# Storing the plain query parts unsplit, a head per store, and splitting them in each attention block

## The chip, the cores and the metric

The kernel runs on one NeuronCore of a Trainium2 chip. The metric is the device time of one execution, in microseconds (us), as the median of several runs; lower is better.

## The reference

One inference step of a two-layer decoder: an mLSTM layer, then a layer of multi-head latent attention (MLA), each followed by a SwiGLU FFN. The change lies in the MLA layer, in the queries of the 1024 prompt tokens and in the attention that reads them:

```python
q = (rmsnorm(c_q, g_q) @ w_uq).reshape(B, S, MLA_HEADS, QK_NOPE + QK_ROPE)   # 8 heads, 128 plain + 64 rotary
q_nope = q[..., :QK_NOPE]
q_rope = rope(q[..., QK_NOPE:], pos)
...
s = q_lat . c_kv + q_rope . k_r          # per head, causal, S = 1024
p = softmax(s * MLA_SCALE)
out = p . c_kv
```

Eight more requests (the sample) each attend, with one token, over 8192 cached positions that are gathered from pages in HBM. All arithmetic is float32.

## The kernel before

TensorE multiplies float32 data as float32r parts: a value x is split into a high part (written by ScalarE as float32r) and the rest (x minus the high part, by VectorE or GpSimd). A product of two split operands is three matmuls: lines 131, 132 and 133 (`mm3`). `split` (line 110) does the two instructions at lines 114 and 115; `split_g` (line 122) is a form that copies PSUM to SBUF on ScalarE first, so that GpSimd can subtract from SBUF (lines 125 to 127).

The MLA layer's part that matters has three stages.

**Queries** (`queries`, line 1307). For each head h the plain part is `P` h: 27 matmuls into three PSUM tiles of 344 tokens ("chunks", 344, 344 and 336 of the prompt). The rotary parts of four heads at a time are `R0` and `R4`: 54 matmuls, then VectorE turns them with the cosines and sines. The order is R0 with P0, P1, P2, P3, R4 with P4, P5, P6, P7 (`ORDER`). Every result chunk is split into an SBUF tile `qx` (two parts) and stored to HBM scratch: plain parts to `qn_d` (line 1331, SP's queue for heads 0 to 3, GpSimd's for the rest), rotary parts to `qr_d` (line 1336, GpSimd's queue for heads 0 to 3, SP's for the rest; two stores for each tile, since a rotary row in `qr_d` holds both parts). There are 12 `qx` buffers and 36 `qx` tiles. `wq` is the weight of all heads (2.36 MB in three loads on SP's queue, line 1319); P1 to P7 and R4 split their weights from it into `wh` and `wl`. R0 and P0 have small loads of their own.

**Sample query** (`sample_query`, line 1406): small matmuls on the eight sample tokens (line 1419 onward, input `qnS`, the last column of each plain part) and ScalarE copies into `qbd` (line 1426). It follows the queries.

**Attention** (`attention`, line 1446). For each of 8 heads there are four blocks G of 256 queries (`prompt`, 32 blocks or slots). A block loads its queries with `load_q` (line 1464) into `q` (both plain parts) and `qrr` (rotary), two buffers each: on ScalarE's queue for head 0, on SP's for the others. Then it does scores (lines 1538 to 1545), the softmax on VectorE and ScalarE (lines 1546 to 1562), transposes and splits of the weights (line 1576 on) and the product with the values (line 1596). Beside the blocks run the next head's keys and values (`head_ops`) and the sample's units (`sample_units`, line 1659): GpSimd gathers pages (`nat`, `nrp`), VectorE transposes them (line 1693), TensorE multiplies (lines 1700 and 1725).

The order on each engine is set by a scheduler, from the order in the code, priorities and its own costs. Each engine then runs its list in order: an instruction that waits holds back all that stand behind it, and this holds for the DMAs that an engine issues.

Of the kernel before, what the change touches and what calls it, by code (L numbers as in the profile page):

```python
# [9 lines left out]
F32 = mybir.dt.float32  # L10
F32R = mybir.dt.float32r
I32 = mybir.dt.int32
AF = mybir.ActivationFunctionType
ALU = mybir.AluOpType
# [4 lines left out]
P = 128  # L19
D = 1024  # L20
KT = D // P
S = 1024
# [3 lines left out]
CW = T // NCH  # L26
# [62 lines left out]
class Kern:  # L89
# [1217 lines left out]
    def queries(self, qs, cq):  # L1307
        nc = self.nc
        V = nc.vector
        cqh, cql, rc, rn, wT = cq  # L1310
        self.qn_d = self.t(self.dp, [8, 2, P, S], "qn_d")
        self.qr_d = self.t(self.dp, [8, P, S], "qr_d")
        wuq = self.mla_w_uq[0]
        self.qnS = self.t(qs, [P, 8, NS], "qnS")
# [1 line left out]

        wq = self.t(qs, [P, 3, 8, 192], "wq")
        for k in range(3):
            nc.sync.dma_start(wq[:, k].rearrange("p h c -> p (h c)"), wuq[k * P:(k + 1) * P, :])


        def keep(c, src, dst, lo_eng=None):
            w = slice(c * CW, min((c + 1) * CW, S))
            n = w.stop - w.start
            x = self.t(qs, [P, 2, CW], "qx", F32R, bufs=12)[:, :, :n]
            self.split(x[:, 0], x[:, 1], src[:, :n], lo_eng=lo_eng)
            return lambda: dst(x.bitcast(F32), w)

        def put_n(h):
            e = nc.sync if h < 4 else nc.gpsimd  # L1330
            return lambda x, w: e.dma_start(self.qn_d[h, :, :, w].rearrange("i p s -> p i s"), x)

        def put_r(h0, e):
            def f(x, w):
# [36 lines left out]
        def plain(h):  # L1371
            raw = wq[:, :, h, 0:P]
            if h == 0:
                raw = self.t(self.wp, [P, KT * P], "wr")[:, : 3 * P].rearrange("p (k m) -> p k m", m=P)
                nc.scalar.dma_start(raw, self.wsrc(wuq, 0, 3, 0, P))
            w = [self.t(self.wp, [P, KT * P], x, F32R)[:, : 3 * P].rearrange("p (k m) -> p k m", m=P) for x in ("wh", "wl")]
            self.split(w[0], w[1], raw)

            def ev(c, cs, ps):
                stores.append(keep(c, ps, put_n(h)))  # L1380
                if c == NCH - 1:
                    V.tensor_tensor(self.qnS[:, h], ps[:, CW - NS:], self.rqS, op=ALU.mult)

            def chunk(c):
                self.linear(w, (cqh, cql), 3, P, ev, chunks=(c,))
                self.lastq = self.last
            return chunk

        stores = []
        for op in ORDER.split():  # L1390
            h = int(op[1:] or 0)
# [54 lines left out]
    def attention(self, ckh, ckl, kk, kl, cqp, cq):  # L1446
        nc = self.nc
# [12 lines left out]
            return r  # L1460

        late = []

        def load_q(h, G):
            g = slice(G * 256, G * 256 + 256)
            q = self.t(pe, [P, 2, 256], "q", F32R, bufs=2)
            x = self.t(pe, [P, 256], "qrr", F32R, bufs=2)
            e = nc.scalar if h == 0 else nc.sync
            e.dma_start(q.bitcast(F32), self.qn_d[h, :, :, g].rearrange("i p s -> p i s"))
            e.dma_start(x.bitcast(F32), self.qr_d[h, :, g])  # L1470
            return q, x

        def head_ops(h):
# [44 lines left out]
        def prompt(h, G, kt, vt):  # L1518
            hv = slice((h % 2) * P, (h % 2) * P + P)
            nk = 2 * G + 2  # L1520
            q, qx = load_q(h, G)
            pt = []
            pn = []
            for i in (2 * G, 2 * G + 1):
                n = (i + 1) * P
# [3 lines left out]
                qs = slice((i % 2) * P, (i % 2) * P + P)  # L1529
# [3 lines left out]
                for c in range(nb):  # L1533
                    w = min(512, n - c * 512)
# [29 lines left out]
            for j0 in range(0, nk, 4):  # L1564
# [3 lines left out]
                for j2 in range(0, m, 2):  # L1568
                    ps = ps1().rearrange("p (j q) -> p j q", q=256)
# [16 lines left out]
            ps = ps1()  # L1586
# [16 lines left out]
        qs = self.pool("qs", side="right")  # L1603
# [13 lines left out]
        for h in range(8):  # L1617
# [11 lines left out]
            for i, G in enumerate(range(4) if h % 2 == 0 or h == 7 else range(3, -1, -1)):  # L1629
                slot = h * 4 + i  # L1630
# [15 lines left out]
        ps = self.tp()  # L1646
# [268 lines left out]
```

## Time and profile before

| what | value |
|---|---|
| median of 3 runs | 2748.43 us (2739.51 to 2748.51) |
| profiled execution | 2769.77 us, 0.78% above the median |
| its span, first to last instruction | 2766.9 us |
| mean granted TensorE clock | 0.972 of full speed |
| busy: PE, PEld, DVE, ACT, POOL | 94%, 88%, 54%, 43%, 32% of the span |
| HBM | 255.17 MB read, 125.70 MB written |
| software queue (GpSimd's), hardware queues | 180.99 MB; 183.61 and 16.36 MB |

PE is TensorE's matmuls and PEld its weight loads, DVE is VectorE, ACT is ScalarE, POOL is GpSimd, SP is SyncE, whose queue only issues DMAs; ACTq and SPq are the DMA issues of those engines. In the rows of the timeline the first column is the start and the second the duration, and brackets give the idle time of the engine ahead of the instruction and what ended it. All times of one view are us from the start of the span. The queries of the MLA layer lie at 1339 to 1411, the attention at 1411 to 1912.

### The profile page before, as it was taken

What the parts mean: (1) busy time and instruction counts of PE and PEld (TensorE: products, weight loads), DVE (VectorE), ACT (ScalarE), POOL (GpSimd) and SP (SyncE); (2) the same over time, 40 slices, a digit from 0 to 9 for tenths busy, and PEclk for the clock granted to TensorE, in tenths of its full rate; (3) what the DMA queues carried; (4) which work ended last, traced back from release to release, by engine and by line L of the source; (5) the groups of instructions that cost most, each with busy time, mean ns of one, the idle gap of its engine ahead of it and who ended that gap; (6) DMA issues with size and microseconds to landing.
All of it is one profiled execution on the core that took longest, in us unless ns stands there. A gap on an engine that the chain in (4) does not pass through costs nothing.

```text
span 2766.9 us, 51992 instructions
## 1 busy us (share of the span) xinstructions
PE 2587.6 (94%) x20719; PEld 2440.0 (88%) x20719; DVE 1491.9 (54%) x3217; ACT 1177.6 (43%) x2651; POOL 875.0 (32%) x843
## 2 busy tenths in 40 slices
PE   8999988989999999999878888898988999999998
PEld 8998877989999999999765667676888999999998
DVE  4345578863334334465546786677574444334455
ACT  4212334544444444453244455546344444444442
POOL 1001002243333333332235444442223333333343
PEclk9999989999999999999889999999999999999999
DMA  5133455426655565453666676654533656555653
GB/s 184 39 76 95 128 140 136 133 69 130 127 118 116 115 123 119 89 178 111 195 209 239 212 249 230 223 204 141 170 100 87 127 116 125 116 117 117 117 138 102
DMA packets 344936, 384.27 MB, mean 139 GB/s; under 512 B 24361, under 2 KB 296110, under 8 KB 336374
## 3 DMA queue, kind: packets, MB, share of 16 engines
q0 software_dynamic: 42064, 180.99, 27.5%
q1 hardware_dynamic: 278422, 183.61, 22.7%
q10 hardware_dynamic: 24208, 16.36, 2.3%
q8 instruction: 162, 2.65, 0.4%
q14 instruction: 80, 0.66, 0.1%
HBM read 255.17 MB, written 125.70 MB: 138 GB/s over the span
## 4 chain that ended last, share of the span: by engine, by line
PE 68%; DVE 13%; DMA 8%; issue 4%; ACT 4%; POOL 2%; SPq 0%; another core or an unknown queue 0%; POOLq 0%; ACTq 0%; DVEq 0%
PE sc L133 10%; PE sc L131 10%; PE sc L132 10%; PE mm L131 5%; PE mm L133 5%; PE mm L132 5%; PE ss L131 5%; PE ss L132 5%; PE ss L133 5%; DVE tt L1693 3%; PE ss L1725 2%; DMA Gb<-G_d 2%; PE ss L1700 2%; DVE wl L115 1%; PE mm L1596 1%
## 5 line engine op out<-in xcount | busy, mean ns | idle before, releaser
L131 PE MATMUL ss<-ah,dh 128*128 128x344 f32 x864 | 277.0, 321 | 6.7 <-ACT st L1075 6.3
L1075 ACT COPY st<-ss 128x344 f32<-128x344 f32 x432 | 189.9, 441 | 214.2 <-PE ss L133 184.1
L132 PE MATMUL ss<-al,dh 128*128 128x344 f32 x864 | 277.0, 321 | 1.9 <-POOL al L115 1.9
L133 PE MATMUL ss<-ah,dl 128*128 128x344 f32 x864 | 276.2, 320 | 0.0
L114 ACT ACTIVATE wh<-wr 128x512 fp32r<-128x512 f32 (+2 forms) x152 | 126.1, 830 | 228.9 <-PE mm L132 130.6
L1077 POOL DMA_DIRECT2D x_d<-st x144 | 124.5, 864 | 241.7 <-ACT st L1075 234.8
L131 PEld LDWEIGHTS ss<-ah,dh 128*128 128x128 f32 x864 | 162.6, 188 | 7.7 <-ACT st L1075 6.7
L132 PEld LDWEIGHTS ss<-al,dh 128*128 128x128 f32 x864 | 163.0, 189 | 2.4 <-POOL al L115 2.4
L115 POOL TENSOR_TENSOR al<-u,ah 128x512 fp32r<-128x512 f32 (+1 forms) x84 | 118.1, 1406 | 148.3 <-ACT ah L114 148.2
L115 DVE TENSOR_TENSOR wl<-S,wl 128x512 fp32r<-128x512 f32 x89 | 78.1, 877 | 157.0 <-ACT wl L114 122.6
L133 PEld LDWEIGHTS ss<-ah,dl 128*128 128x128 f32 x864 | 162.6, 188 | 0.0
L1693 DVE STREAM_TRANSPOSE tt<-nat 128x1024 f32<-128x1024 f32 x128 | 154.0, 1223 | 12.9 <-PE ss L1700 6.3
L115 DVE TENSOR_TENSOR wh<-S,wh 128x512 fp32r<-128x512 f32 x91 | 68.6, 754 | 119.4 <-ACT wh L114 91.2
L1041 DVE TENSOR_TENSOR u<-u,sc 128x260 f32<-128x260 f32 (+1 forms) x168 | 70.8, 421 | 114.7 <-PE sc L133 113.4
L115 DVE TENSOR_TENSOR wl<-wr,wh 128x1024 fp32r<-128x1024 f32 (+2 forms) x83 | 100.5, 1212 | 42.4 <-ACT wh L114 34.8
L1007 POOL TENSOR_TENSOR S<-S,wr 128x512 f32<-128x512 f32 x45 | 62.9, 1397 | 175.3 <-DVE wh L115 87.9
L1700 PE MATMUL ss<-tt,qbd 128*32 128x128 f32 x2560 | 95.6, 285 | 22.5 <-DVE tt L1693 13.7
L1000 POOL TENSOR_TENSOR S<-wr 128x512 f32<-128x512 f32 x45 | 62.0, 1378 | 164.7 <-DMA wr<-in_ffn_w_gate_up_dram 151.5
L131 PE MATMUL mm<-zh,wh 128*128 128x344 f32 x320 | 105.3, 329 | 7.8 <-DVE ot L459 7.8
L1700 PEld LDWEIGHTS ss<-tt,qbd 128*32 128x32 f32 x2560 | 73.7, 114 | 39.1 <-DVE tt L1693 21.2
L115 DVE TENSOR_TENSOR dl<-dr,dh 128x256 fp32r<-128x256 f32 x144 | 69.2, 480 | 72.0 <-ACT dh L114 72.0
L132 PE MATMUL mm<-zl,wh 128*128 128x344 f32 x320 | 104.5, 327 | 0.0
(919 smaller groups left out, 9268.4 us busy)
## 6 DMA issues: line engine op xcount, KB each, us to landing
x_d<-st POOLq DMA_DIRECT2D x144, 516.0 KB
wr<-in_ffn_w_gate_up_dram SPq DMA_DIRECT2D x98, 512.0 KB
dr<-in_ffn_w_down_dram SPq DMA_DIRECT2D x144, 128.0 KB
wr<-in_mlstm_w_in_dram SPq DMA_DIRECT2D x24, 512.0 KB
wr<-in_mlstm_w_out_dram SPq DMA_DIRECT2D x16, 512.0 KB
wr<-in_mla_w_o_dram SPq DMA_DIRECT2D x15, 512.0 KB
q<-qn_d SPq DMA_DIRECT2D x28, 256.0 KB
x_d<-x SPq DMA_DIRECT2D x16, 260.0 KB
```

The costliest lines, as they stand in the source:

```text
L114: ins = nc.scalar.activation(hi, src, AF.Copy)
L115: self.low = e.tensor_tensor(lo, src, hi.bitcast(F32), op=ALU.subtract)
L131: mm(ps, wh, xh, start=start, stop=False, **kw)
L132: mm(ps, wh, xl, start=False, stop=False, **kw)
L133: self.last = mm(ps, wl, xh, start=False, stop=stop, **kw)
L1000: G(s, a21, a22, op=ALU.add)
L1007: G(s, s, a11, op=ALU.subtract)
L1041: V.tensor_tensor(u[:, 1], u[:, 1], ps, op=ALU.add)
L1075: nc.scalar.copy(st[:, cs], ps)
L1077: nc.gpsimd.dma_start(self.x_d[:, d], st, accum_op=ALU.add)
L1693: V.transpose(out=tt, in_=src.rearrange("p s (c i) -> p c s i", i=32))
L1700: nc.tensor.matmul(psS[32 * j:32 * j + 32, u * P:u * P + P], self.qbd[:, b, cb], tt[:, c, 4 * j:4 * j + 4].rearrange("p s k -> p (s k)"), ...
```

## The change

- `qn_d` holds each head's plain part once, unsplit: 8 x 128 x 1024 floats (4 MB, before 8 MB).
- ScalarE copies the three chunks of a head from PSUM into one tile `qp` (128 x 1024, four buffers). When the last is there, the whole head goes out in one store of 128 rows of 4 KB: 8 stores in place of 24. The high part and the rest are no longer made here.
- `qx` serves the rotary parts alone, with 6 buffers in place of 12. The stores of `qr_d` are as they were.
- `load_q` reads the unsplit queries (128 rows of 1 KB) into the second half of `q`; ScalarE writes the high part to the first half (line 1474 of the changed kernel), and GpSimd subtracts in place (line 1475): two more instructions for each of 32 blocks.
- From slot 1 on, the code of a block calls `load_q` for the next block ahead of its own scores; `q` has two buffers as before.
- The three loads of `wq` are issued by GpSimd, no longer by SP.

```diff
-        self.qn_d = self.t(self.dp, [8, 2, P, S], "qn_d")
+        self.qn_d = self.t(self.dp, [8, P, S], "qn_d")
...
-            nc.sync.dma_start(wq[:, k].rearrange("p h c -> p (h c)"), wuq[k * P:(k + 1) * P, :])
+            nc.gpsimd.dma_start(wq[:, k].rearrange("p h c -> p (h c)"), wuq[k * P:(k + 1) * P, :])
...
-            x = self.t(qs, [P, 2, CW], "qx", F32R, bufs=12)[:, :, :n]
+            x = self.t(qs, [P, 2, CW], "qx", F32R, bufs=6)[:, :, :n]
...
-        def put_n(h):
-            e = nc.sync if h < 4 else nc.gpsimd
-            return lambda x, w: e.dma_start(self.qn_d[h, :, :, w].rearrange("i p s -> p i s"), x)
...
+            x = self.t(qs, [P, S], "qp", bufs=4)
             def ev(c, cs, ps):
-                stores.append(keep(c, ps, put_n(h)))
+                w = slice(c * CW, min((c + 1) * CW, S))
+                nc.scalar.copy(x[:, w], ps[:, :w.stop - w.start])
                 if c == NCH - 1:
+                    stores.append(lambda: (nc.sync if h < 4 else nc.gpsimd).dma_start(self.qn_d[h], x))
...
-            e.dma_start(q.bitcast(F32), self.qn_d[h, :, :, g].rearrange("i p s -> p i s"))
+            raw = q[:, 1].bitcast(F32)
+            e.dma_start(raw, self.qn_d[h, :, g])
             e.dma_start(x.bitcast(F32), self.qr_d[h, :, g])
+            nc.scalar.activation(q[:, 0], raw, AF.Copy)
+            nc.gpsimd.tensor_tensor(q[:, 1], raw, q[:, 0].bitcast(F32), op=ALU.subtract)
...
-            q, qx = load_q(h, G)
+            slot = h * 4 + G if h % 2 == 0 or h == 7 else h * 4 + 3 - G
+            q, qx = ahead.pop(slot, None) or load_q(h, G)
+            n = slot + 1
+            if 0 < slot < 31:
+                ahead[n] = load_q(n // 4, n % 4 if n // 4 % 2 == 0 or n >= 28 else 3 - n % 4)
```

What the scheduler makes of it, at three places. The rows show line, operation and tiles (output, arrow, inputs) in the order in which the engine runs them; the numbers in names tell buffers apart.

ScalarE in the queries, before, from the third split of R0's and P0's chunks on. `qrr` and `q` are the queries of slots 0 and 1, and `wh <- wq` are the weights of P1 and P2:

```order
L114 ACTIVATE qx_14512<-rfa_14507 128x344
L1470 DMA qrr_15078<-qr_d_14414 128x256
L114 ACTIVATE qx_14520<-rfa_14515 128x344
L114 ACTIVATE qx_14533<-sc_14523 128x344
L114 ACTIVATE wh_14598<-wq_14417 128x384
L114 ACTIVATE wh_14657<-wq_14417 128x384
L1469 DMA q_15077<-qn_d_14413 128x2x256
L114 ACTIVATE qx_14561<-rfa_14556 128x336
L1470 DMA qrr_15236<-qr_d_14414 128x256
```

The same place in the changed kernel, from P2's weights (the first row; P1's stand two rows ahead of it) to P3's (the last row):

```order
L114 ACTIVATE wh_14645<-wq_14417 128x384
L1473 DMA qrr_15024<-qr_d_14414 128x256
L114 ACTIVATE qx_14572<-rfa_14567 128x336
L1472 DMA q_15023<-qn_d_14413 128x256
L1472 DMA q_15181<-qn_d_14413 128x256
L1380 COPY qp_14597<-sc_14598 128x344
L1473 DMA qrr_15182<-qr_d_14414 128x256
L1380 COPY qp_14597<-sc_14609 128x344
L1474 ACTIVATE q_15023<-q_15023 128x256
L1474 ACTIVATE q_15181<-q_15181 128x256
L1380 COPY qp_14597<-mm_14620 128x336
L114 ACTIVATE wh_14685<-wq_14417 128x384
```

The weights of P1 and P2 have moved ahead of the first query load; both loads and the splits of slots 0 and 1 now stand between them and P3's weights.

GpSimd's list at the start of the queries, before (`cn_d` is a small store of the stage ahead):

```order
L1282 DMA cn_d_14301<-so_14297 8x256
L1336 DMA qr_d_14414<-qx_14463 4x32x344 x2
L1336 DMA qr_d_14414<-qx_14471 4x32x344 x2
L1336 DMA qr_d_14414<-qx_14512 4x32x344 x2
L1336 DMA qr_d_14414<-qx_14520 4x32x344 x2
```

and in the changed kernel:

```order
L1282 DMA cn_d_14301<-so_14297 8x256
L1319 DMA wq_14417<-in_mla_w_uq_dram 128x1536 x3
L1332 DMA qr_d_14414<-qx_14464 4x32x344 x2
L1332 DMA qr_d_14414<-qx_14472 4x32x344 x2
L1332 DMA qr_d_14414<-qx_14511 4x32x344 x2
L1332 DMA qr_d_14414<-qx_14519 4x32x344 x2
```

The three loads of `wq` now stand on this queue, ahead of R0's stores.

ScalarE in the attention, before, at the end of head 1 (`wr` are softmax rows, `ot` a block's output, `vt` the next head's values):

```order
L1560 ACTIVATE wr_16512<-wr_16512,sm_16502 128x128
L1555 ACTIVATE wr_16527,sm_16517<-sc_16518,mx_16516,rqt_14290 128x256
L1560 ACTIVATE wr_16527<-wr_16527,sm_16517 128x256
L1599 COPY ot_16419<-mm_16406 128x256
L1601 DMA ot_d_14312<-ot_16419 128x256
L125 ACTIVATE vt_16422<-mm_16423 128x512
```

and in the changed kernel:

```order
L1570 ACTIVATE wr_16478<-wr_16478,sm_16468 128x128
L1750 ACTIVATE fac_16661<-fac_16661 128x1
L1570 ACTIVATE wr_16493<-wr_16493,sm_16483 128x256
L1474 ACTIVATE q_16837<-q_16837 128x256
L1609 COPY ot_16383<-mm_16370 128x256
L1611 DMA ot_d_14312<-ot_16383 128x256
L125 ACTIVATE vt_16386<-mm_16387 128x512
```

The split of a later block's queries stands ahead of the copies that empty PSUM.

More of the change, by code (lines that the diff above doesn't have):

```diff
@@ L1462, in attention @@
         late = []
+        ahead = {}
         def load_q(h, G):
```

## The prediction

> **What bounds the kernel now.** I read the page first (busy shares, granted clock, chain), then stretches of the time line around the edit, then the waits inside them.
>
> ```profile
> PE 2587.6 (94%) x20719; PEld 2440.0 (88%) x20719; DVE 1491.9 (54%) x3217; ACT 1177.6 (43%) x2651; POOL 875.0 (32%) x843
> PEclk9999989999999999999889999999999999999999
> PE 68%; DVE 13%; DMA 8%; issue 4%; ACT 4%; POOL 2%; SPq 0%; another core or an unknown queue 0%; POOLq 0%; ACTq 0%; DVEq 0%
> ```
>
> TensorE bounds the whole. The clock row dips only around the middle, where the queries and the start of the attention lie, so the edit is worth what TensorE idles, or runs slowly, there. The stretches (length, then busy us of PE, PEld, DVE, ACT, POOL with instruction counts, then granted clock, DMA share, GB/s):
>
> ```profile
> 1349.00:1357.00 8.00, 0.04 (x1) 0.00 (x0) 0.77 (x2) 1.29 (x4) 0.51 (x1) 0.65 0.68 217
> 1357.00:1366.00 9.00, 8.49 (x31) 8.05 (x32) 4.11 (x14) 0.85 (x2) 2.17 (x4) 0.55 0.58 144
> 1380.00:1396.00 16.00, 15.84 (x100) 15.56 (x100) 15.29 (x47) 6.43 (x15) 4.08 (x6) 1.00 0.65 195
> 1396.00:1411.00 15.00, 7.58 (x57) 7.49 (x55) 2.94 (x10) 2.25 (x5) 3.28 (x6) 0.84 0.57 195
> 1411.00:1430.00 19.00, 16.59 (x79) 12.99 (x79) 4.42 (x20) 11.32 (x29) 2.79 (x4) 0.68 0.38 136
> 1430.00:1912.00 482.00, 412.44 (x5083) 325.45 (x5084) 338.94 (x745) 249.65 (x660) 217.77 (x213) 0.95 0.64 219
> ```
>
> A full-speed matmul of the queries takes 16.0/100 = 0.16 us. There are two holes, 1349 to 1357 and before 1411, each followed by a stretch at about half clock. The attention itself is 86% PE-busy (412.44 of 482) and full speed. ScalarE's and TensorE's time lines name the causes:
>
> ```profile
> 1355.32 0.34 ACTq L1470 DMA_DIRECT2D qrr<-qr_d  x1
> 1355.71 0.49 ACT L114 ACTIVATE qx<-rfa 128x344 fp32r<-128x344 f32 x1 [9.01 <-DMA qr_d<-qx]
> 1366.20 0.48 ACT L114 ACTIVATE qx<-rfa 128x336 fp32r<-128x336 f32 x1 [8.02 <-DMA qr_d<-qx]
> 1409.64 0.46 ACT L114 ACTIVATE qx<-sc 128x344 fp32r<-128x344 f32 x1 [7.86 <-DMA qr_d<-qx]
> 1357.01 0.65 PE L131 MATMUL sc<-cqh,wh 128*128 128x344 f32 x1 [7.97 <-ACT wh L114]
> 1401.91 1.68 PE L1419 MATMUL ss<-qnS,wT 128*128 128x8 f32 x14
> 1411.19 4.01 PE L1419 MATMUL ss<-qnS,wT 128*128 128x8 f32 x18 [7.61 <-DVE qnS L1382]
> ```
>
> The first hole is ScalarE standing in slot 0's rotary load, which waits for R0's first-chunk stores, while P1's weight split stands behind it. At 1366 it has waited for slot 1's load in the same way. At 1409.64 it waits for a `qx` buffer whose rotary store has not landed, and P7's last pieces, with `qnS`, come late.
>
> **The change, part by part.**
>
> *First hole.* P1's weights now stand ahead of the load; they need only `wq` and the copy of P0's last chunk.
>
> ```profile
> 1340.62 2.25 SPq L1319 DMA_DIRECT2D wq<-in_mla_w_uq_dram  x3
> 1337.58 0.50 POOL L1282 DMA_DIRECT2D cn_d<-so  x1
> 1350.00:1352.00 2.00, 0.00 (x0) 0.00 (x0) 0.00 (x0) 0.00 (x0) 0.00 (x0) 0.87 1.03 364
> 1352.00:1354.00 2.00, 0.00 (x0) 0.00 (x0) 0.00 (x0) 0.00 (x0) 0.00 (x0) 0.50 0.58 127
> L114 ACT ACTIVATE qx<-sc x16: 439/457/487, 1344.5 to 1409.6; 128x344 fp32r<-128x344 f32 x16
> L115 DVE TENSOR_TENSOR qx<-sc,qx x16: 501/508/517, 1345.2 to 1410.1; 128x344 fp32r<-128x344 f32 x16
> L1331 POOL DMA_DIRECT2D qn_d<-qx x12: 725/725/761, 1381.3 to 1411.7; - x12
> ```
>
> GpSimd is free at 1338.1, 2.5 us before SP issued the same loads. Three issues of 0.73 us and 2.36 MB at 364 GB/s (6.5 us) put `wq` in SBUF near 1347. TensorE ends P0 at 1349.0; a copy and a split of some 0.45 us each give P1's start at 1350.3. The wait falls from 7.97 to 1.3: gain 6.7. The ends are 8.0 (no wait) and 4.9 (if `wq` lands only where the rate fell, at 1352, P1 starts by 1352.1).
>
> *Half clock after it.* The 31 matmuls of 1357 to 1366 took 9.0 us where 31 x 0.16 = 5.0 would do: gain 4.0 when the hole goes, 0 if another hole of that size follows.
>
> *The wait that may replace it.* P3's weights now stand behind slot 1's rotary load, which needs all eight stores of R0's chunks 0 and 1.
>
> ```profile
> 1357.15 8.60 DMA qr_d<-qx
> 1380.68 27.48 SPq L1336 DMA_DIRECT2D qr_d<-qx  x12
> 1404.00:1406.00 2.00, 0.00 (x0) 0.00 (x0) 0.00 (x0) 0.00 (x0) 0.00 (x0) 1.00 0.67 223
> 1406.00:1408.00 2.00, 0.00 (x0) 0.00 (x0) 0.00 (x0) 0.00 (x0) 0.00 (x0) 0.52 0.27 94
> 1408.00:1410.00 2.00, 0.00 (x0) 0.00 (x0) 0.00 (x0) 0.36 (x2) 0.00 (x0) 0.50 0.26 86
> ```
>
> The chain shows that the last of the eight needed 8.60 us from issue to landing. ScalarE no longer stops ahead of that chunk, so its stores are issued by about 1349.5 and land near 1358.1; the load, two copies, two query splits and the weight split (about 2.6 us) put P3 at 1360.7. TensorE has P1 and P2 meanwhile, 54 x 0.16 = 8.6 us, to 1358.9. New wait 1.8. The ends: 0, and 9.0 if the stores go one behind the other, since SP's twelve took 27.48 / 12 = 2.29 us each: eight from 1347 land at 1365.3, P3 at 1367.9. I take 1.8, because the 8.60 is the row of this very store.
>
> The Trainium skill ("DMA: Bandwidth & Descriptors", section on why a DMA increments its semaphore by 16) says that a DMA uses as many engines, at most 16, as divide its slowest dimension, which is four heads for a rotary store: the lowest four from SP, and from GpSimd four consecutive ones from a moving cursor. The trace agrees for SP: a DMA share of 0.26 and 0.27 is four engines of 16. No row here shows the cursor; by that rule GpSimd's stores run beside each other, the new wait is 0 and the sum 1.8 larger.
>
> The Trainium skill ("TensorE: Matmul & The Clock Gate", Part 1) lets the clock drop after an idle window of about 3.4 us. The trace agrees: TensorE went idle at 1403.6, the clock was 1.00 to 1406 and 0.52 after it. By that rule a wait of 1.8 costs no clock, and one of 9.0 does.
>
> *Second hole.* `qx` is used by 12 rotary tiles with 6 buffers, so R4 needs what R0 stored over 20 us before; `qp` has four buffers, and P4 to P7 need the stores of P0 to P3, which stand on SP's queue ahead of the slow rotary ones. ScalarE does not stop and the 7.61 go. The ends are 7.6 and 0 (if a `qp` store comes late). I take 7.6, since SP's queue holds nothing else then. The 18 multiplications at line 1419 took 4.01 us where 14 had taken 1.68: 1.85 from the clock alone; up to 1430 the mean clock was 0.68, at most 0.32 x 19 = 6.1. I take 3.0, nearer the lower end, because ScalarE (11.32 of 19) paces that stretch.
>
> *Work removed from the queries.* 24 subtractions of 0.51 us on VectorE (12 us) and 4 MB of stores. TensorE, at 15.84 of 16 in the stretch from 1380, covers them: 0. The 24 copies replace 24 splits on ScalarE at the same 0.45.
>
> *Work added to the attention.*
>
> ```profile
> 1422.44 0.39 ACT L114 ACTIVATE wh<-mm 128x256 fp32r<-128x256 f32 x1 [1.04 <-PE mm L1576]
> 1317.69 0.90 POOL L222 TENSOR_TENSOR rq<-rq,sq 128x344 f32<-128x344 f32 x1 [0.25 <-ACT sq L221]
> L1538 PE MATMUL sc<-kt,q 128*128 128x512 f32 (+3 forms) x72 | 29.2, 406 | 4.8 <-DMA q<-qn_d 3.3 <-ACT wr L1555 1.4
> 1784.90 5.51 DMA q<-qn_d
> 1667.51 0.36 SPq L1469 DMA_DIRECT2D q<-qn_d  x1
> 1667.86 0.30 PE L1538 MATMUL sc<-kt,q 128*128 128x128 f32 x1
> 1674.41 0.28 PE L1538 MATMUL sc<-kt,q 128*128 128x128 f32 x1
> ```
>
> 32 splits of 0.39 are 12.5 us on ScalarE; 32 subtractions of 0.90 x 256/344 = 0.67 are 21.4 us on GpSimd. Loading ahead in the code brings nothing by itself: with two buffers SP already issues a load as soon as the block before last is read (1667.51, as the block at 1667.86 begins; used at 1674.41), and one wait of 3.3 us is all that TensorE had from queries; its load took 5.51 us. What changes is that ScalarE now stands in its list until the load has landed, with PSUM copies, softmax rows and the next weights queued behind it, and GpSimd until ScalarE is done, with the gathers behind it. If neither is ever late, the loss is -3.3 (the one wait goes); if both are wholly on the path, 33.9. I take 8: ScalarE is busy 249.65 of 482 us, so 52% of its 12.5, or 6.5, delays something, and 1.5 for the few blocks as tight as the one at 1674. GpSimd I cost at 0, covered by its own idle time (217.77 busy of 482); if that cover goes, gathers come late.
>
> *Sum.* 6.7 + 4.0 - 1.8 + 7.6 + 3.0 = 19.5 gained in the queries, 8 lost in the attention: 11.5. Against the profiled 2769.8 that is 2758; the profiled run lies 0.78% above the median of 2748.4, and from the median it is 2737.
>
> **Rivals.**
>
> *Nothing is paid in the attention* (loss near -1): the splits fall into ScalarE's idle half. For it: loads had 7 us of slack even at 1667.51. Against it: that same load needs 5.51, and then two engines in turn. Gain 20.5: 2728.
>
> *The rotary stores are still late.* Eight at 2.29 us each: the new wait is 9.0 in place of 1.8, and the half clock comes back, 4.0. Gain 0.3: 2748, no change. For it: SP's row. Against it: the stores before 1355 went beside the saturated `wq` load. From 3.4 us of new wait on it starts to tell.
>
> *ScalarE in the queries' way*, slower: if in the 14 short blocks (G 0 and 1, outside head 0) TensorE pays a third of the landing, 1.8 us, and in 14 others the 0.39 and 0.67 in full, that is 25.2 + 14.8 = 40, against 19.5: 2769. It decides beyond 1.2 us a block, (19.5 + 13.7) / 28. For it: the third place in the lists, where a split stands ahead of PSUM copies. Against it: TensorE's list also holds the sample's work there.
>
> **How the numbers follow.** A measurement of this kernel can tell about 0.5%, 13.7 us. Forecast 0.42, with a range of its own of 2729 to 2744; nothing paid 0.27; stores still late 0.20; slower rival 0.09; the remaining 0.02 goes to slower for what I do not see. Below 2734.7 lie the second case and a third of the first: faster 0.42. Same: the rest of the first and the third, 0.47. Slower 0.11. The range reaches from the free attention with the larger clock term (2728 less the 3.1 between 3.0 and 6.1, and a run's scatter of some 5) to between the late stores and the slower rival: 2719 to 2760.
>
> **What would show it.** Right: PE's wait for P1's `wh` under 2 us; the wait ahead of P3 under 3; no wait at the sample's `qnS`; clock 1.00 through the queries; the sample's first products (line 1420) running through near 1395 instead of stopping until 1411. In the attention: PE idle up from 70 us to under 80, ScalarE's waits for `q` loads of 1 to 4 us. Wrong: a hole of 9 us ahead of P3, or ScalarE waits at line 1474 that sum past 30 us with PE idle growing alike.

## The result and the profile after

The changed kernel takes 2758.22 us (median of 16 runs, 2745.08 to 2765.31) against 2745.29 for the kernel before (16 runs): a ratio of 1.0043, 95% interval 1.0032 to 1.0055. The forecast was 0.996. In a second session the ratio was again 1.0043.

One thing has to be said before profiles are compared: chips differ. In the sessions that follow the kernel before took 2769, 2773, 2751, 2748 and 2769 us, on five chips. The profile shown in the prediction (span 2766.9, attention 560.5 us) is like the slower chips; the profile of after, below, was taken in a session like the faster ones. The kernel before was therefore profiled twice more, once on a chip of each kind. In the experiments each ratio is of runs on one chip.

Page of the changed kernel:

```profile
PE 2581.8 (94%) x20719; PEld 2436.3 (88%) x20719; DVE 1491.0 (54%) x3193; ACT 1186.8 (43%) x2683; POOL 894.0 (32%) x870
PEclk9999989999999999999989989998999999999999
```

The same stretches as in the prediction, in the changed kernel (length, busy us of PE, PEld, DVE, ACT and POOL, granted clock, DMA share, GB/s):

```profile
1349.00:1357.00 8.00, 4.73 (x27) 3.88 (x26) 3.09 (x11) 0.48 (x1) 1.51 (x3) 1.00 0.81 181
1357.00:1366.00 9.00, 3.37 (x21) 3.08 (x20) 0.00 (x0) 1.69 (x5) 0.79 (x2) 0.81 0.49 118
1366.00:1380.00 14.00, 13.21 (x66) 12.93 (x67) 6.18 (x15) 5.55 (x14) 1.10 (x2) 0.76 0.29 114
1380.00:1396.00 16.00, 16.00 (x103) 15.97 (x102) 12.31 (x42) 6.42 (x15) 1.18 (x2) 1.00 0.47 133
1396.00:1411.00 15.00, 15.00 (x101) 13.38 (x100) 2.96 (x14) 5.82 (x13) 2.44 (x4) 0.75 0.71 202
1411.00:1430.00 19.00, 15.52 (x56) 11.73 (x55) 4.81 (x15) 14.79 (x37) 7.67 (x8) 0.66 0.33 101
```

The hole of 1349 to 1357 has become smaller, a new one has opened in 1357 to 1366 (PE busy 3.37 of 9), and the clock that was low up to 1366 is now low up to 1380. Before the sample (1396 to 1411) TensorE no longer stops.

Two stretches that do not depend on fixed times tell the sum: from the first matmul of the queries to the sample's last product, and from there to the last score of the output projection with `zh0h` (the attention). The kernel before on a chip of the faster kind, then the changed kernel:

```profile
1321.20:1416.30 95.10, 78.93 (x468) 75.86 (x468) 52.67 (x151) 28.71 (x63) 27.15 (x38) 0.85 0.63 194
1416.30:1949.60 533.30, 475.13 (x5433) 380.07 (x5433) 370.61 (x812) 286.94 (x740) 242.45 (x241) 0.94 0.65 225
```

```profile
1319.30:1405.30 86.00, 74.84 (x468) 71.06 (x469) 42.88 (x127) 29.49 (x65) 22.78 (x35) 0.93 0.55 157
1405.30:1964.40 559.10, 481.97 (x5432) 384.49 (x5433) 381.69 (x812) 294.41 (x770) 264.44 (x272) 0.93 0.61 208
```

The queries gained 9.1 us and the attention lost 25.8. Of the 25.8, 19.0 are idle time of TensorE (77.1 against 58.2, length minus busy) and 6.8 are the same matmuls taking longer at a lower mean clock. Of the 9.1, 5.0 are idle time (11.2 against 16.2) and 4.1 matmul time.

TensorE's time line in the queries of the changed kernel, the rows with a wait, and the sample's products:

```profile
1347.55 0.42 PE L131 MATMUL sc<-cqh,wh 128*128 128x344 f32 x1 [0.95 <-ACT wh L114]
1356.80 0.43 PE L133 MATMUL sc<-cqh,wl 128*128 128x344 f32 x1 [2.79 <-DVE wl L115]
1366.79 0.65 PE L131 MATMUL sc<-cqh,wh 128*128 128x344 f32 x1 [6.42 <-ACT wh L114]
1400.84 4.45 PE L1420 MATMUL ss<-qnS,wT 128*128 128x8 f32 x32
```

and what ScalarE does ahead of P3 (1366.79):

```profile
1354.38 0.35 ACTq L1473 DMA_DIRECT2D qrr<-qr_d  x1
1354.78 0.48 ACT L114 ACTIVATE qx<-rfa 128x336 fp32r<-128x336 f32 x1 [6.49 <-DMA qr_d<-qx]
1360.17 1.37 ACTq L1472 DMA_DIRECT2D q<-qn_d  x2
1361.77 0.33 ACTq L1473 DMA_DIRECT2D qrr<-qr_d  x1
1365.20 0.79 ACT L1474 ACTIVATE q<-q 128x256 fp32r<-128x256 f32 x2 [2.62 <-DMA q<-qn_d]
1366.21 0.52 ACT L114 ACTIVATE wh<-wq 128x384 fp32r<-128x384 f32 x1
```

P1 starts 0.95 us after P0 (7.97 before). Then ScalarE stands in slot 0's rotary load until 1354.38, in the loads of the first two query tiles until 1360.17, and at their splits until these have landed, 1365.20. By the code the loads at 1360.17 read what P0 stored, the whole head in one store that SP issued at 1347.10. Slot 1's rotary load, at 1361.77, comes after that. P3's weights (1366.21) stand behind all of it.

The waits in the attention of the changed kernel, 1430 to 1890 (sum, times, longest):

```profile
POOL q L1475 <- ACT q L1474: 62.5, 17, 7.2
ACT q L1474 <- DMA q<-qn_d: 46.9, 17, 8.5
POOL wl L127 <- ACT spl L126: 42.5, 17, 15.4
POOL vt L127 <- ACT spl L126: 18.2, 7, 4.7
POOL kt L127 <- ACT spl L126: 16.7, 7, 5.6
```

ScalarE waits 2.8 us at a time for queries to land, and GpSimd with it. GpSimd also waits for ScalarE at `split_g`'s subtractions (line 127): 42.5 + 18.2 + 16.7 = 77 us here, 127 in a kernel without splits in the attention (below). I read these waits as its slack, of which standing at the queries (62.5 us) has used up the 50 between them; no run shows that the one replaced the other.

### The profile page after: what moved, and what is told of

Its sections match the earlier page's. It is cut to its first block, busy times and chain, and to the rows that moved or that the text cites. A ratio compares the mean times of both kernels' runs of the same rounds, so it can differ in the third digit from the quotient of the medians.

```text
span 2756.6 us, 52000 instructions
## 1 busy us (share of the span) xinstructions
PE 2581.8 (94%) x20719; PEld 2436.3 (88%) x20719; DVE 1491.0 (54%) x3193; ACT 1186.8 (43%) x2683; POOL 894.0 (32%) x870
## 3 DMA queue, kind: packets, MB, share of 16 engines
q0 software_dynamic: 41856, 181.26, 27.9%
## 5 line engine op out<-in xcount | busy, mean ns | idle before, releaser
L133 PE MATMUL mm<-zh,wl 128*128 128x344 f32 x320 | 104.4, 326 | 0.0
L1710 PE MATMUL ss<-tt,qbd 128*32 128x128 f32 x2560 | 90.9, 284 | 12.6 <-DVE tt L1703 10.5
```

The source lines that it names most:

```text
L133: self.last = mm(ps, wl, xh, start=False, stop=stop, **kw)
L1710: nc.tensor.matmul(psS[32 * j:32 * j + 32, u * P:u * P + P], self.qbd[:, b, cb], tt[:, c, 4 * j:4 * j + 4].rearrange("p s k -> p (s k)"), ...
```

## The experiments

A ratio is to the kernel before, on the same chip, by the runs of the same session.

**The kernel before, again.**

> The kernel before, unchanged, profiled once more. The first profile of it is of an execution of 2769.8 us, 24 us over the median of its runs (2745.3), so what that profile shows may not be usual. Theory A, the hole ahead of the sample's work is unusual: the sample's products (line 1419) run through within 3 us of 1402, where they broke off until 1411, and 8 to 14 of the 24 us are gone there. Theory B, the holes are usual and the excess lies in the attention: line 1419 breaks off as it did, and the last score of the attention is at about 1890 in place of 1911.6. Theory C, the same profile and another 2770: then profiled executions of this kernel are slow, and the comparison of the two profiles (11 us for the change) says nothing of unprofiled ones.

The span was 2763.5, on a chip where the kernel takes 2769 in the median. The two stretches:

```profile
1319.50:1414.70 95.20, 79.06 (x468) 75.94 (x468) 52.48 (x151) 28.81 (x63) 27.72 (x38) 0.85 0.62 193
1414.70:1971.70 557.00, 484.47 (x5433) 383.67 (x5433) 372.84 (x813) 286.28 (x740) 242.83 (x241) 0.94 0.63 216
```

None of the three theories: the sample's products broke off as before, the last score was at 1903.9, and the profile was usual for its chip. So the first profile's 24 us over the median are most likely the chip: its attention took 560.5 us, near the 557.0 here. The record does not name the chip of that profile.

**wq on GpSimd, alone.**

```
-            nc.sync.dma_start(wq[:, k]...
+            nc.gpsimd.dma_start(wq[:, k]...
```

> The kernel before with one part of the change: the three loads of wq issued by GpSimd in place of SP. If wq was late for P1 (its weights), the hole of 7.97 us ahead of P1 shrinks by the 2 to 3 us that wq comes earlier: 2742 to 2744. If ScalarE's stand in the rotary load alone sets the hole, nothing changes: 2745, within 3. Rival, the earlier wq takes the DMA engines from the first rotary stores or delays them on GpSimd's list by its three issues: up to 5 slower, 2750.

0.9984 (0.9969 to 0.9999), 4.4 us. The hole ahead of P1 went from 7.67 (the run above) to 5.09, within the 2 to 3 us of the first theory. That `wq` had been late is not shown by this, since the order on ScalarE changed too: P1's weights (1357.52) now stand behind the load of slot 0's plain part (1356.97), and the rotary load comes after them (1359.06).

**No load ahead.**

```
-            if 0 < slot < 31:
+            if False:
```

> The changed kernel with the loads and splits of a block's queries at the start of that block, not a block ahead. Theory 1, the splits placed a block ahead stall ScalarE (46.9 us of waits at them in the profile) and that is the loss: the splits then wait too, but directly ahead of the block that needs them; faster than the changed kernel by 5 to 13 us, 2745 to 2753. Theory 2, being ahead hides the landing (about 3 to 5 us a block) and the splits (1.1 us in turn): without it the changed kernel gets slower by 28 blocks x 1 to 2 us, 2786 to 2814.

1.0027 (1.0009 to 1.0045): nominally 4 us better than the changed kernel, with intervals that overlap. Loading ahead in the code hides nothing, and it is not shown to be the loss either.

**No split in the attention** (both halves are the unsplit query; 32 copies on ScalarE and 32 subtractions on GpSimd left out):

```
-            e.dma_start(raw, self.qn_d[h, :, g])
+            e.dma_start(q.bitcast(F32), self.qn_d[h, :, g].unsqueeze(1).to_broadcast([P, 2, 256]))
...
-            nc.scalar.activation(q[:, 0], raw, AF.Copy)
-            nc.gpsimd.tensor_tensor(q[:, 1], raw, q[:, 0].bitcast(F32), op=ALU.subtract)
```

> The changed kernel without the splits in the attention: both halves of a query tile are loaded from the unsplit query (as many bytes as before loaded), so the low half is wrong and 32 copies on ScalarE and 32 subtractions on GpSimd are left out. What is left of the change is its part in the queries. Theory 1, the loss is ScalarE and GpSimd in the attention: faster than before by what the queries gained, 2730 to 2740. Theory 2, the loss is in the queries (ScalarE now stands in loads of the plain part ahead of P3's weights, a hole of 6.4 us, with the wait of 2.8 before it): as the changed kernel, 2752 to 2760.

0.9963 (0.9947 to 0.9979), 10.2 us faster. So the splits cost (1.0043 - 0.9963) x 2769 = 22 us, and what is left of the change gains 10. Not all of the 22 lies in the attention: the splits of slots 0 and 1 stood in the queries, where the waits ahead of P2 and P3 are now 1.37 + 3.03 = 4.4 us in place of 9.2 (7.4 in the changed kernel's second profile, on a chip of this kind). In its profile the attention is as long as before on that chip, and GpSimd waits longer at `split_g`:

```profile
1322.20:1404.00 81.80, 75.75 (x468) 72.06 (x469) 42.18 (x127) 28.51 (x63) 21.66 (x32) 0.94 0.56 169
1404.00:1960.90 556.90, 483.71 (x5433) 385.36 (x5433) 379.77 (x812) 285.72 (x740) 242.87 (x242) 0.94 0.64 216
POOL wl L127 <- ACT spl L126: 75.0, 17, 23.6
POOL vt L127 <- ACT spl L126: 31.0, 7, 8.8
POOL kt L127 <- ACT spl L126: 20.9, 6, 5.7
1360.75 0.43 PE L133 MATMUL sc<-cqh,wl 128*128 128x344 f32 x1 [1.37 <-DVE wl L115]
1367.37 0.42 PE L131 MATMUL sc<-cqh,wh 128*128 128x344 f32 x1 [3.03 <-ACT wh L114]
```

**The changed kernel again, and each engine's half alone.** ScalarE's half is the changed kernel without the subtraction; GpSimd's half loads both halves unsplit and leaves the copy out:

```
-            nc.gpsimd.tensor_tensor(q[:, 1], raw, q[:, 0].bitcast(F32), op=ALU.subtract)      # ScalarE alone
...
-            e.dma_start(raw, self.qn_d[h, :, g])                                              # GpSimd alone
+            e.dma_start(q.bitcast(F32), self.qn_d[h, :, g].unsqueeze(1).to_broadcast([P, 2, 256]))
-            nc.scalar.activation(q[:, 0], raw, AF.Copy)
```

> The changed kernel, unchanged, timed and profiled beside the others, since the kernel before took 2745 us in one session and 2769 in the next: chips differ, and only profiles of one session can be laid side by side. The ratio should come back as 1.003 to 1.0055. On a chip where the kernel before takes 2769, its queries end (last matmul with cqh) within 2 us of the kernel before, its sample products end 8 to 10 us earlier (near 1405 in place of 1414), and the way from there to the end of the attention and the output projection is 18 to 25 us longer than in the kernel before (556.5 us from the sample's last product at 1414.3 to the last zh0h score at 1970.8).

> The changed kernel without the 32 subtractions on GpSimd (the low half stays the unsplit query, so the scores are wrong); ScalarE's 32 copies and their waits stay. Theory 1, ScalarE that stands for the landing is the loss: within 4 us of the changed kernel, ratio 1.002 to 1.006. Rival, GpSimd's 0.74 us, with the gathers of the sample queued behind it (it waited 62.5 us at them), is the loss: near the run without either, 0.996 to 0.999.

> The changed kernel without the 32 copies on ScalarE (both halves loaded unsplit, the low one then made by GpSimd's subtraction; the scores are wrong); ScalarE has no work and no wait for queries. Theory 1, ScalarE is the loss: near the run without either, 0.996 to 0.999. Rival, GpSimd is the loss: 1.002 to 1.006. If both runs lie in the middle, the loss is shared.

1.0043 (1.0028 to 1.0057); ScalarE alone 0.9986 (0.9976 to 0.9997); GpSimd alone 1.0036 (1.0022 to 1.0050). Against no split, which was timed on another chip, ScalarE's half costs 0.0023 x 2773 = 6.4 us (the two intervals leave 1 to 12), GpSimd's 0.0073 x 2773 = 20 us (14 to 26), both 22. The rival held: most of it is GpSimd. The attention in the three, first the changed kernel, then ScalarE alone and GpSimd alone, all on one chip of the slower kind (557.0 and 560.5 in the two profiles of the kernel before):

```profile
1407.30:1990.60 583.30, 497.73 (x5433) 393.97 (x5433) 379.38 (x812) 294.97 (x770) 265.21 (x272) 0.92 0.59 200
1409.80:1982.60 572.80, 493.42 (x5433) 388.37 (x5433) 371.13 (x812) 293.93 (x770) 242.98 (x242) 0.92 0.60 203
1402.90:1988.20 585.30, 499.01 (x5432) 392.95 (x5433) 387.53 (x813) 284.92 (x740) 265.05 (x273) 0.92 0.60 206
```

The changed kernel's attention is 26.3 us longer than the 557.0, a little over the 18 to 25 that were expected. ScalarE alone takes 12 to 16 us more there than the kernel before, more than its 6.4 by the times; that profile is of its slowest run, 5.8 us over its median.

**The subtraction on VectorE.**

```
-            nc.gpsimd.tensor_tensor(q[:, 1], raw, ...
+            V.tensor_tensor(q[:, 1], raw, ...
```

> The changed kernel with the 32 subtractions on VectorE in place of GpSimd. So far: without any split in the attention 0.9963 of the kernel before, ScalarE's copies alone 0.9986, GpSimd's subtractions alone 1.0036, both 1.0043. Theory P, GpSimd's list is what costs (it stands until queries have landed, with the low halves of split_g and the sample's gathers behind): 0.998 to 1.001. Theory O, any instruction put into the attention gives another order of issue there (the scheduler's lists of all engines change at a few hundred places) and that costs: 1.002 to 1.006 here too. Rival, VectorE is the busier engine (70% of the stage) and 32 x 0.3 us on it cost as much: 1.002 to 1.005.

1.0051 (1.0031 to 1.0071). Theory P fails: off GpSimd's list the loss is no smaller. VectorE stood 27.9 us behind ScalarE's splits, and the attention took 570.2 on a chip of the faster kind (533.3 in the kernel before). Theory O and the rival, that VectorE is the busier engine, give the same range, so this run does not tell them apart.

```profile
1403.20:1973.40 570.20, 488.92 (x5432) 390.88 (x5433) 384.66 (x842) 296.26 (x770) 243.10 (x242) 0.92 0.60 204
DVE q L1475 <- ACT q L1474: 27.9, 13, 5.2
```

**The waits without the work, and the work without the waits for a DMA.** The first splits one column of 256:

```
+            raw = q[:, 1, 0:1].bitcast(F32)
+            nc.scalar.activation(q[:, 0, 0:1], raw, AF.Copy)
+            nc.gpsimd.tensor_tensor(q[:, 1, 0:1], raw, q[:, 0, 0:1].bitcast(F32), op=ALU.subtract)
```

> The run without splits in the attention, with both split instructions put back for one column of 256: they stand in the lists of ScalarE and GpSimd and wait for the landing as in the changed kernel, and do next to no work (the scores stay wrong). Theory W, the waits for the landing are the loss: 1.002 to 1.005. Theory K, the work of the two instructions (0.42 and 0.74 us a block) is the loss: 0.996 to 0.998, as without any split.

The second puts a subtraction of full size on GpSimd behind each block's first softmax sum:

```
                 V.reciprocal(sm[:, 0:1], sm[:, 0:1])
+                if i == 2 * G:
+                    nc.gpsimd.tensor_tensor(self.ct[:, C_SI:C_SI + 256], self.ct[:, 0:256], sm[:, 0:1].to_broadcast([P, 256]), op=ALU.subtract)
```

> The run without splits in the attention, with 32 subtractions of the same size on GpSimd that read a constant and the block's softmax sum (so that they stand in the block) and write where nothing reads: the work of GpSimd without a wait for a DMA. Theory W, the wait for the landing is the loss: 0.996 to 0.999. Theory K or O, the work or the changed order is: 1.001 to 1.005.

1.0033 (1.0016 to 1.0049) for the waits without work, 0.9982 (0.9962 to 1.0002) for GpSimd's work without a wait for a DMA. Both on one chip of the faster kind, the first two rows the one column, the others GpSimd's work:

```profile
1410.70:1968.90 558.20, 485.17 (x5433) 387.18 (x5433) 371.30 (x812) 288.22 (x770) 247.63 (x272) 0.92 0.63 215
POOL q L1475 <- ACT q L1474: 78.8, 20, 12.0
```

```profile
1410.50:1956.60 546.10, 480.74 (x5433) 385.23 (x5433) 381.34 (x812) 285.20 (x740) 264.71 (x275) 0.93 0.65 220
POOL ct L1567 <- DVE sm L1565: 32.6, 16, 10.6
```

One column costs (1.0033 - 0.9963) = 0.0070 (0.0047 to 0.0093) of the 0.0080 that the whole split costs; GpSimd's full work in another place costs 0.0019, with an interval that holds 0 and ends at 0.0045. So most of the loss comes without the work: it is that instructions stand in the lists where they stand. Two things limit this. GpSimd's work has a wait of its own, 32.6 us for VectorE, and its attention is 13 us longer than the 533.3 of the kernel before, half of what the one column adds (25). And of the 13 us by which the run with one column is the slower of the two (2758.8 against 2745.7), 4 lie in the queries (86.5 against 82.5), where only it stands at the landing of the first two tiles.

**Splits placed later.** First by moving them in the code to the end of the block before, then with an explicit edge as well:

```
             for j0 in range(0, nk, 4): ...
+            if slot + 1 in ahead:
+                with self.tc.issue_after(lastpx.ins):        # the second kernel only
+                    split_q(ahead[slot + 1][0])
             ps = ps1()
```

> The changed kernel with the loads a block ahead as they are, and the two split instructions of the next block moved in the code from the head of the block before to its end (behind its softmax and transposes). Theory 1, the loss is engines that stand in their lists until a load has landed: the loads have landed by then, so most of the loss goes, 0.996 to 1.000 of the kernel before. Theory 2, the loss is the work itself on ScalarE and GpSimd (0.42 and 0.74 us a block), or TensorE that waits for the split: as the changed kernel, 1.002 to 1.006.

> The changed kernel with the two split instructions of the next block bound by an explicit edge behind the last exponential of the block before (in split_late the scheduler could still put them ahead, and ScalarE waited 41 us at them). The loads stay a block ahead. Theory W, the wait for the landing is the loss: ScalarE's waits at the splits fall under 15 us and the ratio to 0.997 to 1.000. Rival, TensorE now waits for the splits instead (its scores of the next block stand right behind): 1.002 to 1.010, with PE waits at the scores (sc<-kt,q) above 20 us.

1.0027 (1.0013 to 1.0042) and 1.0159 (1.0140 to 1.0178). In the first the scheduler still put most of them early. In the second they stand behind the last exponential, ScalarE hardly waits for landing, and yet the loss is larger. So ScalarE's wait for the landing, theory W, does not explain the loss by itself; GpSimd still stands 47.2 us behind the splits. The rival's range was passed and its sign did not come: TensorE's direct waits for ScalarE at the scores are 10.3 us, where over 20 were expected, of the 52 us by which the attention is longer than the 533.3.

```profile
1408.30:1993.70 585.40, 495.77 (x5433) 399.90 (x5433) 376.12 (x812) 299.44 (x770) 264.97 (x272) 0.91 0.58 199
PE sc L1554 <- ACT q L1478: 10.3, 7, 1.8
```

Neither of these two places between a landing and the scores that need it was free.

**Splits stored by the queries.** A head is stored at once, both halves, from two buffers:

```
-            x = self.t(qs, [P, S], "qp", bufs=4)
+            x = self.t(qs, [P, 2, S], "qp", F32R, bufs=2)
...
-                nc.scalar.copy(x[:, w], ps[:, :w.stop - w.start])
+                self.split(x[:, 0, w], x[:, 1, w], ps[:, :w.stop - w.start])
```

> A version that keeps what the change does in the queries and not what it does in the attention: the plain parts are split in the queries as before (24 subtractions on VectorE), a whole head's two halves are stored at once in 4-KB rows, loads are as before but a block ahead, wq by GpSimd, two buffers a head's size. If the queries' gain holds (0.9963 without splits in the attention) and VectorE's 24 subtractions there are covered: 0.995 to 0.998. If two buffers make ScalarE wait for stores: 0.998 to 1.001.

0.9982 (0.9964 to 0.9999). The attention is the old one (536.8 us on a chip of the faster kind), and in this profile, of a run 7.5 us over its median, the queries took 96.0, with 2.84 and 3.77 us of waits ahead of P2's last weights and P3's:

```profile
1331.30:1427.30 96.00, 83.65 (x468) 79.36 (x468) 51.90 (x151) 28.31 (x63) 22.32 (x32) 0.84 0.59 186
1427.30:1964.10 536.80, 472.24 (x5433) 379.20 (x5433) 375.66 (x812) 285.43 (x740) 243.22 (x242) 0.95 0.65 225
```

**Rotary stores on 128 rows**, without and with the first loads on GpSimd:

```
-        self.qr_d = self.t(self.dp, [8, P, S], "qr_d")
+        self.qr_d = self.t(self.dp, [2, 2, 2, P, S], "qr_d")
...
-   ...dma_start(self.qr_d[h0:h0 + 4, 64 * i + 32 * e:64 * i + 32 * e + 32, w], x[:, i])
+   ...dma_start(self.qr_d[h0 // 4, i, e, :, w], x[:, i])
...
-            e = nc.scalar if h == 0 else nc.sync                                # the second kernel only
+            e = (nc.gpsimd if G < 2 else nc.scalar) if h == 0 else nc.sync
```

> The version with stored splits (0.9982), and the rotary queries stored in another order in DRAM, so that a store's outermost dimension is 128 rows and not 4 heads. Theory S, the rotary stores are late because each runs on four DMA engines: the two waits ahead of P2's and P3's weights (2.84 and 3.77 us) go, 4 to 9 us faster than that version: 0.995 to 0.997. Rival, ScalarE stands in its loads for the heads' own stores: both waits stay, 0.998.

> As the run before (stores on 128 rows), and the query loads of the first two blocks issued by GpSimd, so that ScalarE stands in none of them. If the loads that stand in ScalarE's list are what holds P2's and P3's weights, their waits go here at the latest: 0.993 to 0.996. If nothing of the two was left after the run before: the same as it within 2 us.

0.9991 (0.9973 to 1.0009) and 0.9985 (0.9968 to 1.0001). Theory S holds in its place: the waits ahead of P2 and P3 are gone, the queries take 76.0 us, and it does not matter which engine issues the loads (76.4). The median store from GpSimd lands in 4.6 us where it took 11.5 in the version with stored splits, the first row:

```profile
qr_d<-qx POOLq DMA_DIRECT2D x8, 172.0 KB, 11.5
```

```profile
1318.70:1394.70 76.00, 73.25 (x468) 69.89 (x468) 52.28 (x151) 29.02 (x63) 21.17 (x33) 0.97 0.67 246
qr_d<-qx POOLq DMA_DIRECT2D x8, 172.0 KB, 4.6
PE sc L1549 <- DMA qrr<-qr_d: 18.9, 5, 8.6
```

The head's own store follows: ScalarE's load of P0's queries goes out 17.5 us after that store was issued in the version with stored splits (1363.73 to 1381.22) and 7.6 us after it here (1348.96 to 1356.58), with nothing changed but the order of the rotary parts. The last row is where the gain went: now the rotary loads are the narrow ones, and TensorE waits 18.9 us for them in the attention (560.1 us against 536.8).

**The kernel before, on the faster kind of chip.**

> The kernel before, for a profile on the same chip. From the last of the sample's products to the last zh0h score the stage takes 537 us if this is a chip where the kernel takes 2745 to 2751, as it did in the version with stored splits (536.8), and 556 on one where it takes 2769; a half clock of 50 to 55 us or of 65 in that stage goes with it.

533.3 us, as shown with the result: the two chips differ in the attention; ahead of the queries, in them, and behind the attention the two profiles differ by less than 2 us each.

**Neither narrow.** Stores on 128 rows and each rotary load in four pieces of 32 rows, on the version with stored splits, then on the kernel before with nothing else changed:

```
+            r = 32 * (h % 4)
+            for k in range(4):
+                e.dma_start(x[32 * k:32 * k + 32].bitcast(F32), self.qr_d[h // 4, k // 2, k % 2, r:r + 32, g])
```

> As rot16 (splits stored by the queries, rotary stores on 128 rows), with each block's rotary load in four pieces of 32 rows. If both the holes of the queries and the late rotary loads came from DMAs that run on few engines: the queries stay at 76 us from their first matmul to the sample's last product (95 in the kernel before), TensorE's wait for qrr falls from 18.9 to under 4 us, and the time is 0.991 to 0.995 of the kernel before. If four loads on SP's queue are late themselves: 0.998 to 1.001 as in rot16.

> The kernel before with nothing changed but the order of the rotary queries in DRAM: stores on 128 rows, loads in four pieces. If its two holes (7.6 to 8.0 us each, with half a clock behind them) are the rotary stores: both under 2 us and 0.992 to 0.996. If ScalarE still stands in a load ahead of P1's weights because of the heads' own stores or of wq: the first hole stays over 4 us, the second goes, 0.996 to 0.999.

0.9932 (0.9915 to 0.9950), 18.8 us faster than the kernel before, the best of all, with 2.6 us left of TensorE's 18.9 for the rotary loads; and 0.9980 (0.9968 to 0.9992). The first two rows are the former, the last two the latter, on one chip of the slower kind:

```profile
1318.70:1395.00 76.30, 73.74 (x468) 70.58 (x469) 52.95 (x151) 28.89 (x63) 20.90 (x33) 0.95 0.66 241
1395.00:1954.00 559.00, 476.87 (x5432) 377.58 (x5433) 372.95 (x812) 286.10 (x740) 242.12 (x241) 0.95 0.63 215
```

```profile
1321.30:1400.90 79.60, 73.25 (x468) 70.39 (x469) 53.12 (x151) 29.34 (x63) 25.29 (x38) 0.96 0.69 236
1400.90:1977.70 576.80, 494.94 (x5433) 395.76 (x5433) 374.74 (x812) 285.46 (x740) 242.22 (x241) 0.92 0.61 208
```

In the kernel before the queries fall from 95 to 79.6 by the rows alone, with 5.42 us left ahead of P1. But its attention grows from 557 to 576.8 with no split in it, 9.3 us of idle time and 10.5 of matmul time. Between the two kernels here TensorE's idle time is equal (82.1 and 81.9), and the 18 us are the same matmuls taking longer, at a clock of 0.92 against 0.95. The four-piece loads changed the order: by the traces some 330 of ScalarE's 2760 other instructions stand elsewhere than in the kernel before, and some 60 in the version with stored splits against the same version with whole loads.

**What stays open.** In the splits' case two things come together that no kernel here separates: engines that stand at the split until a landing, and another order of all lists, which the scheduler makes as soon as anything is added to the attention. GpSimd's work with a changed order but no such wait cost 0.0019; the two kernels with four-piece loads do the same work in the attention, and differ there by 18 us at equal idle time. How much moves does not tell the price: against the run without splits, 269 of ScalarE's 2764 instructions stand elsewhere in the run with GpSimd's work (0.0019), 375 with ScalarE's half (0.0023), 325 with one column (0.0070) and 422 in the changed kernel (0.0080), counted in the traces. That the loss comes with the splits, and most of it not with their work, is shown; how the 20 us divide between wait and order is not.

## Why the prediction was wrong, point by point

- **First hole, gain 6.7.** Right: 7.97 became 0.95, a gain of 7.0.
- **Half clock after it, gain 4.0.** Came in part: a hole of 6.42 us followed, ending at 1366.79, and the clock was 0.81 and 0.76 in the two stretches around it. The 66 matmuls of 1366 to 1380 took 13.21 us where 66 x 0.16 = 10.6 would do: 2.6 lost, in place of 4.0. The text had the condition ("0 if another hole of that size follows").
- **The wait that may replace it, 1.8.** The first failed step: 2.79 + 6.42 = 9.2 us. The term that was priced was nearly right: the eight rotary stores were to land at 1358.1, and by the trace their last packet ended at 1357.3. What the working left out is what else ScalarE stands in ahead of P3's weights: until 1360.17 for P0's own store, and until 1365.20 for the landing of the two plain loads; only the work of the splits was counted. Without splits in the attention the two waits are 1.37 + 3.03 = 4.4. The end of 9.0 met the measured 9.2 by luck: its eight stores one behind the other would have landed at 1365.3, but slot 1's rotary load went out at 1361.77, and the price of 2.29 us came from SP's stores, where the packets of GpSimd's eight took 12.7 us (1344.6 to 1357.3), 1.6 each. The prediction's inference from the Trainium skill ("DMA: Bandwidth & Descriptors", section on why a DMA increments its semaphore by 16), that GpSimd's stores run beside each other so that the wait would be 0, failed too as a price. The rule of the Trainium skill there, that the slowest dimension sets the number of engines, agrees with the stores on 128 rows, 4.6 us against 11.5.
- **Second hole, gain 7.6.** Right: the sample's products run through from 1400.84 to 1405.29, and no wait stands ahead of them.
- **Clock after it, 3.0.** Less than half of it came: the 32 products of the sample took 4.45 us, before 1.68 + 4.01 = 5.69. The reason given failed: with no hole ahead of the sample (TensorE busy in all 15 us from 1396) the clock fell all the same, to 0.75 there and 0.66 from 1411 to 1430 (0.68 before).
- **The queries together.** Forecast 6.7 + 4.0 - 1.8 + 7.6 = 16.5, measured 9.1 in the profile. The 7.4 between them is what the wait ahead of P2 and P3 was too short by. With the stores on 128 rows and the splits left in the queries the gain is 95.1 - 76.0 = 19.1: the forecast's holes were the right ones, and what held them open was the rotary stores, by themselves and through the head's store that ran beside them. The third case, given 0.20, had named these stores.
- **ScalarE in the attention, 8.** Near in size, 6.4 us by the times (1 to 12). That is luck in part: 6.5 of the 8 was a share of the splits' work, and one column, with next to no work, cost nearly as much as whole splits. Its waits of 2.8 us each lie in the 1 to 4 that were named, but their sum, 46.9 us, is past the 30 that the text gave as a sign of being wrong.
- **GpSimd in the attention, 0.** The step that decided the sign. It was said to be covered by GpSimd's idle time, and the text named what goes if the cover goes. The idle time was no cover for an instruction that makes the engine stand: with GpSimd 45% busy, its instruction of 0.74 us in each block cost 20 us, and the one-column split lost nearly as much with next to none.
- **Loading ahead brings nothing.** Borne out: 1.0027 without it.
- **From the profile to the median.** The 0.78% by which the profiled run lay above the median was taken as scatter; most likely it was the chip. The terms did not suffer, since the queries are equally long on both kinds.
- **The rivals.** The late stores came true in their place, and their price (9.2 for 9.0) by another sum, as said. The slower one, engines in the way of each other in the attention, came true in sign at 22 us for the 40 that it priced, and was given 0.09. It let TensorE pay the landing and the work; most of the loss came without the work, and GpSimd was the larger part.

## What to carry to other kernels

Do not cover an instruction that waits for a DMA with its engine's idle share; ask what stands behind it on its engine, and what order a scheduler will make of it. Here an engine that was 45% busy gave no cover, and one column of the split cost nearly as much as the whole. Before work is moved to fill a hole, ask what holds the hole open: here it was the shape of the stores. With the splits left in the queries, whole-head stores, `wq` on GpSimd and loads ahead gave 0.9982 together, and turning the rotary parts' outermost dimension from 4 to 128 rows, with loads in pieces, brought this to 0.9932 (on another chip); the same turning on the kernel before gave 0.9980. When an edit lets a scheduler reorder everything, time a version of it that does no work.

## What the runs showed of the hardware that was not expected

- The chips of these sessions fall into two kinds for this kernel, 2745 to 2751 and 2769 to 2773 us, and in one profile of each kind the 24 us lie in the attention alone (533.3 against 557.0).
- In the attention a quarter to a half of what the change costs is not idle time but clock: 6.8 of 25.8 us on the faster kind. On the slower kind the changed kernel has 13.1 us more of idle time than the kernel before (85.6 against 72.5) and 13.3 us more of busy time for the same matmuls. No long hole did this: the clock's records come in steps of 3.41 us, and in the two profiles on the faster kind (10 and 9 drops) the step ahead of a drop held no gap of TensorE longer than 2.83 us. The longest gap was 0.66 us in one of them, TensorE was busy for 0.17 to 0.62 of most of these steps, and in each profile one drop followed a step that was busy throughout. So the prediction's reading that a wait of 1.8 us costs no clock does not carry over to the attention.
